# Feed-forward layers: one 512-column product for a weight's high part, with the sum's halves added outside

## The chip, the core and the metric

One core of a Trainium2 chip runs the whole kernel as one program. The metric is the device time of one execution in microseconds. TensorE (PE) multiplies; VectorE (DVE), ScalarE (ACT) and GpSimd (POOL) do the rest; SyncE (SP) issues most of the DMA.

## The reference

Two transformer blocks over 256 tokens of width 1024 (float32). The first block has two layers, each a feed-forward layer, a mixing layer (a causal convolution, then latent attention), and a second feed-forward layer. The second block mixes tokens by a gated recurrence and attention over a context, and ends in 16 experts.

```python
def swiglu_ffn(h, w1, w3, w2):
    return (jax.nn.silu(h @ w1) * (h @ w3)) @ w2

def first_block(x, ...):                # D_MODEL 1024, D_FF 2816
    h = x
    for i in range(DEPTH):              # 2
        h = h + 0.5 * swiglu_ffn(rmsnorm(h, ffn_norm1[i]), ffn1_w1[i], ffn1_w3[i], ffn1_w2[i])
        m = rmsnorm(h, mix_norm[i])
        h = h + (conv_module(m, ...) if i % 2 == 0 else mla(m, ...))
        h = h + 0.5 * swiglu_ffn(rmsnorm(h, ffn_norm2[i]), ffn2_w1[i], ffn2_w3[i], ffn2_w2[i])
    return rmsnorm(h, final_norm)
```

So there are four feed-forward layers; each reads 3 x 1024 x 2816 weights.

## The kernel before

**Products in three parts.** A float32 product is made of float32r products: the weight is split into a high part whi and a low part wlo, the activation into xh and xl, and `mm3` adds whi xh (L301), whi xl (L302) and wlo xh (L303) in one PSUM region. Features lie on partitions, the 256 tokens along the free axis, and a [128, 128] tile of the weight is stationary, so each product has 256 moving columns and the three of a triple load the stationary operand three times.

**The weights' stream.** `Stream` loads chunks of up to 1 MB, mostly [128, 8, 256], into a ring of raw buffers in the order of use. A chunk is used in two parts. For each part ScalarE copies the high part (L193, whi) and VectorE subtracts for the low part (L197, wlo); four pairs of buffers hold parts ahead of their use, and a part's pair is refilled when TensorE is through with it. These splits are issued between the products, and so stand in the queues of ScalarE and VectorE at written-out places.

**A feed-forward layer** (`ffn`, L551). For each of 11 pairs of hidden blocks there is a gate projection pg (w1) and an up projection pu (w3): two column blocks of 128, 8 k each, into one PSUM bank [128, 2 x 256] (`proj_pair`). Then VectorE multiplies pg by rb, the tokens' 1 / rms (L569), ScalarE takes Silu (L570), GpSimd multiplies by rb again (L571), VectorE multiplies with pu (L573), and `split_act` makes hh on ScalarE (L338) and hl on VectorE (L340). `out_proj` (L527) then takes 22 k for 8 output blocks, two at a time, each in a bank of its own (pd). For each output block `done` adds it to h on VectorE (L491; L489 in the mixing layers; L1174 in the last layer), and makes the next layer's xh (L492) and xl (L493).

**Order.** The schedule is as written: each engine works its instructions in program order. Fillers, small pieces of other work such as the second block's context, are put at set places (`FILL1`, `FILL3`: after each hidden pair, after each output block). Among them are the context's transposes, four turns of a bank ctr (L1060) that VectorE reads twice each (hc, L1063).

**PSUM.** Of eight banks, five take turns for products (`bank`), two serve small sums (`psx`) and one the conditions and the like (`psf`). A tile waits for the last reader of the tile that had its bank before.

Of the kernel before, what the change touches and what calls it, by code (L numbers as in the profile page):

```python
# [17 lines left out]
P = 128  # L18
# [7 lines left out]
# vectors brought in as rows of 128 and transposed on the chip: name -> first row, rows  # L26
# [10 lines left out]
# f32 inverse frequencies, ROPE_THETA ** (-2 i / 64) and ROPE_THETA ** (-2 i / 32)  # L37
# [4 lines left out]
def hmask(p):  # L42
    """pairs (s, c) of a 32 x 32 block that halves of blocks of 2, 4, ... 32 split, both ways"""
    s, c = p[:, None] % 32, np.arange(32)[None, :]
    lv = []
    for b in (1, 2, 4, 8, 16):
        same = s // (2 * b) == c // (2 * b)
        lv.append(same & (s // b < c // b))
        lv.append(same & (s // b > c // b))
    return np.concatenate(lv, 1).astype(np.float32)  # L50


def constants():
    """Arrays that depend on shapes alone, side by side in one [128, n] array."""
# [76 lines left out]
class Chunk:  # L131
    """A piece of a weight, [128, k, f]; its split parts are used in order, once each."""
# [6 lines left out]
    def parts(self):  # L139
        """(first k, number of k, (hi, lo)) for each part"""  # L140
# [5 lines left out]
class Stream:  # L146
    """Weights in the order in which they are used: loaded as far ahead as the rings have room,
    and those for float32r products split into a high and a low part, n_hl parts ahead."""
# [15 lines left out]
    def add_ring(self, pool, n):  # L164
        """n more buffers"""
        self.rings.append([pool, n, 0])
# [16 lines left out]
    def spare(self):  # L183
        """a buffer, when all is loaded"""
# [22 lines left out]
    def ahead(self, n):  # L207
        """the high parts of the next n splits, where they are loaded; -> what makes the low ones"""
# [29 lines left out]
    def drop(self):  # L238
        """the chunk that was got last is used up"""
# [9 lines left out]
    def get(self, k, f, load, split=True):  # L249
        """the next chunk; all that were got before are used up"""  # L250
# [11 lines left out]
def wcols(name, idx, c0, n, k0=0, nk=None):  # L262
    """Chunk: rows k0*128.. (nk tiles), columns c0..c0+n of a [K, N] weight."""
# [11 lines left out]
def wq_heads(g):  # L275
    """Heads 2g and 2g+1 of the query weight: 128 + 128 columns without, 64 + 64 with rotation."""
# [8 lines left out]
def two(a):  # L285
    """[128, 512] as [128, 2, 256]"""
# [3 lines left out]
class Kernel:  # L290
# [8 lines left out]
    def mm3(self, ps, w, x, start, stop, **kw):  # L299
# [3 lines left out]
        mm(ps, w[1], x[0], start=False, stop=stop, **kw)  # L303

# [30 lines left out]
    def split_act(self, hi, lo, src, scale=1.0):  # L335
        """scale * src (f32) -> hi + lo in float32r, exactly (scale: a power of two)."""
# [33 lines left out]
    def rstd_from_sum(self, sums, n, c=2):  # L370
        """sums [128, c] (PSUM or SBUF): -> [128, c] of 1 / sqrt(sum / n + eps)"""
# [4 lines left out]
    def warm(self, func):  # L376
        """brings in the function's table"""
# [3 lines left out]
    def rsqrt(self, m, c):  # L381
# [4 lines left out]
        # one Newton step takes the square root's table to float32's accuracy  # L386
# [24 lines left out]
    def bcast(self, r, dg=None):  # L411
        """r [128 tok, 2] -> [128, 256] with r along the free axis, in PSUM"""
# [7 lines left out]
    def apply_norm(self, src, rb, gain, xh, xl, nk, func=None, shift=None, new=None):  # L420
        """func(src[:, k] * gain(k) * rb) or that + shift(k) -> hi + lo"""
# [23 lines left out]
    def new_act(self):  # L445
        xh = self.actp.tile([P, KD, T], F32R, name="xh", tag="xh")
        xl = self.actp.tile([P, KD, T], F32R, name="xl", tag="xl")
        return xh, xl
# [1580 lines left out]
```

## Time and profile before

| | |
|---|---|
| time, median of 3 runs | 1829.04 us (1826.76 to 1830.6) |
| span of the profiled execution | 1826.4 us |
| mean granted TensorE clock | 0.937 |
| first feed-forward layer | about 11 to 218 us |
| convolution | about 218 to 399 us |
| second and third feed-forward layer | about 399 to 782 us |
| latent attention | about 782 to 900 us |
| fourth feed-forward layer | about 900 to 1091 us |
| second block up to the experts | 1091 to 1340 us |
| experts | 1340 to 1826 us |

The stages' ends are read from the first matmul of each. A granted clock of 1.00 is TensorE's upper level, 2.4 GHz. A matmul's record is longer than the distance to the next one's start, since matmuls are pipelined; what one costs in a dense stretch is the distance of the starts. In a row, the text in square brackets is the idle time before the instruction and what ended it.

### The profile page before, as it was taken

Reading aid. Unit: us, or ns where it says so; the run is one execution under the profiler, and the core shown is the slowest. Engines: PE = TensorE matmul, PEld = TensorE weight load, DVE = VectorE, ACT = ScalarE, POOL = GpSimd, SP = SyncE. Lnnn points to the kernel's source line nnn. Section 1 sums busy time; section 2 is a strip of 40 time slices with the busy share of each in tenths; the row PEclk is TensorE's granted clock in tenths of the full one; section 3 lists DMA queues with packets and bytes.
Section 4 is the critical chain, followed back from the end, with each engine's and each line's share of the span. In section 5 each row is a group of like instructions: output and inputs, shape, how many; then the busy total and the mean of one; then the engine's idle time right before and its main releaser. Section 6 shows DMA issues by size and latency. Waiting matters only on the chain.

```text
span 1826.4 us, 32080 instructions
## 1 busy us (share of the span) xinstructions
PE 1628.4 (89%) x13567; PEld 1376.9 (75%) x13567; DVE 921.3 (50%) x1470; ACT 696.2 (38%) x1082; POOL 229.2 (13%) x222
## 2 busy tenths in 40 slices
PE   8999989799999999999999999988988866766765
PEld 8998988689999999987999999877973421322322
DVE  5555689965555655564665536876641110101101
ACT  5454465464444544444544445545431000000001
POOL 0112067411100111010011020310010000000000
PEclk9999998899999999999999999999988988877876
DMA  8767733335556565566755558332889999999997
GB/s 266 224 225 261 227 119 113 94 112 182 184 175 201 164 197 174 172 191 221 226 175 183 172 181 252 106 99 80 307 330 372 408 409 409 409 409 408 409 409 279
DMA packets 262891, 435.40 MB, mean 238 GB/s; under 512 B 15466, under 2 KB 203548, under 8 KB 260700
## 3 DMA queue, kind: packets, MB, share of 16 engines
q1 hardware_dynamic: 262188, 431.52, 67.3%
q8 instruction: 106, 1.74, 0.4%
q0 software_dynamic: 528, 1.84, 0.3%
q14 instruction: 37, 0.30, 0.1%
q10 hardware_dynamic: 32, 0.01, 0.0%
HBM read 432.27 MB, written 1.05 MB: 237 GB/s over the span
## 4 chain that ended last, share of the span: by engine, by line
PE 59%; DMA 23%; DVE 13%; ACT 3%; issue 2%; SPq 0%; POOL 0%; DVEq 0%; ACTq 0%; POOLq 0%
DMA raw<-in_w_exp_up_dram 16%; PE mm L301 12%; PE mm L303 12%; PE mm L302 12%; DMA raw<-in_w_exp_down_dram 6%; PE pd L301 6%; PE pd L302 6%; PE pd L303 6%; DVE cv L663 4%; DVE wlo L197 2%; PE gu L1725 1%; ACT whi L193 1%; PE mod L948 1%; PE xe L1684 1%; DMA raw<-in_ffn_w_dram 0%
## 5 line engine op out<-in xcount | busy, mean ns | idle before, releaser
L197 DVE TENSOR_TENSOR wlo<-raw,whi 128x1024 fp32r<-128x1024 f32 (+1 forms) x381 | 456.9, 1224 | 203.4 <-ACT whi L193 202.5
L303 PE MATMUL mm<-xh,wlo 128*128 128x256 f32 (+1 forms) x1888 | 537.4, 285 | 6.6 <-DVE wlo L197 6.6
L301 PE MATMUL mm<-xh,whi 128*128 128x256 f32 (+1 forms) x1888 | 540.1, 286 | 3.3 <-ACT whi L193 3.0
L302 PE MATMUL mm<-xl,whi 128*128 128x256 f32 (+1 forms) x1888 | 537.1, 284 | 0.4 <-DVE xl L431 0.3
L193 ACT ACTIVATE whi<-raw 128x1024 fp32r<-128x1024 f32 (+1 forms) x381 | 382.3, 1031 | 190.2 <-PE mm L302 83.7
L301 PEld LDWEIGHTS mm<-xh,whi 128*128 128x128 f32 (+1 forms) x1888 | 364.7, 193 | 9.1 <-ACT whi L193 3.6
L303 PEld LDWEIGHTS mm<-xh,wlo 128*128 128x128 f32 (+1 forms) x1888 | 364.4, 193 | 8.0 <-DVE wlo L197 8.0
L302 PEld LDWEIGHTS mm<-xl,whi 128*128 128x128 f32 (+1 forms) x1888 | 364.6, 193 | 0.8 <-DVE xl L431 0.5
L1725 PE MATMUL gu<-raw,xe 128*32 128x512 f32 x1024 | 158.4, 718 | 59.6 <-DMA raw<-in_w_exp_up_dram 59.5
L301 PE MATMUL pd<-hh,whi 128*128 128x256 f32 x704 | 199.6, 284 | 1.3 <-DVE hc L1063 1.3
L302 PE MATMUL pd<-hl,whi 128*128 128x256 f32 x704 | 199.2, 283 | 0.0
L303 PE MATMUL pd<-hh,wlo 128*128 128x256 f32 x704 | 199.2, 283 | 0.0
L1725 PEld LDWEIGHTS gu<-raw,xe 128*32 128x32 f32 x1024 | 26.4, 116 | 150.2 <-issue 144.9
L301 PEld LDWEIGHTS pd<-hh,whi 128*128 128x128 f32 x704 | 135.1, 192 | 4.0 <-issue 2.3
L302 PEld LDWEIGHTS pd<-hl,whi 128*128 128x128 f32 x704 | 135.1, 192 | 0.0
L303 PEld LDWEIGHTS pd<-hh,wlo 128*128 128x128 f32 x704 | 135.1, 192 | 0.0
L1737 DVE TENSOR_TENSOR mhd<-gu,msg 128x256 f32<-128x256 f32 x16 | 6.8, 425 | 232.3 <-ACT msg L1733 232.3
L1754 PE MATMUL dn<-raw,mht 128*32 128x256 f32 x1024 | 85.8, 489 | 32.6 <-DMA raw<-in_w_exp_down_dram 18.2
L571 POOL TENSOR_TENSOR sg<-sg,rbs 128x512 f32<-128x512 f32 x44 | 56.7, 1288 | 450.5 <-ACT sg L570 450.5
L1754 PEld LDWEIGHTS dn<-raw,mht 128*32 128x32 f32 x1024 | 35.3, 135 | 80.5 <-DMA raw<-in_w_exp_down_dram 36.0
L1733 ACT ACTIVATE msg<-gu 128x256 f32<-128x256 f32 x16 | 6.1, 383 | 219.7 <-PE gu L1725 219.7
L475 POOL TENSOR_TENSOR ssum<-ssum,sq 128x256 f32<-128x256 f32 x48 | 37.8, 794 | 362.2 <-ACT sq L474 362.2
(447 smaller groups left out, 2126.3 us busy)
## 6 DMA issues: line engine op xcount, KB each, us to landing
raw<-in_ffn_w_dram SPq DMA_DIRECT2D x120, 1024.0 KB
raw<-in_w_exp_gate_dram SPq DMA_DIRECT2D x128, 512.0 KB
raw<-in_w_exp_up_dram SPq DMA_DIRECT2D x128, 512.0 KB
raw<-in_w_exp_down_dram SPq DMA_DIRECT2D x64, 1024.0 KB
raw<-in_w_in_dram SPq DMA_DIRECT2D x28, 1024.0 KB
raw<-in_w_mod_dram SPq DMA_DIRECT2D x24, 1024.0 KB
raw<-in_ffn_w_dram SPq DMA_DIRECT2D x16, 768.0 KB
raw<-in_conv_w_pw_dram SPq DMA_DIRECT2D x12, 1024.0 KB
```

The costliest lines, as they stand in the source:

```text
L193: nc.scalar.activation(hi, r, AF.Copy)
L197: eng.tensor_tensor(lo, r, hi.bitcast(F32), op=ALU.subtract)
L301: mm(ps, w[0], x[0], start=start, stop=False, **kw)
L302: mm(ps, w[0], x[1], start=False, stop=False, **kw)
L303: mm(ps, w[1], x[0], start=False, stop=stop, **kw)
L475: (eng or nc.vector).tensor_tensor(ssum, ssum, s, op=ALU.add)
L571: nc.gpsimd.tensor_tensor(two(sg), two(sg), rb, op=ALU.mult)
L663: self.nc.vector.scalar_tensor_tensor(acc, src, g, acc, op0=ALU.mult, op1=ALU.add)
L948: nc.tensor.matmul(ps[32 * j:32 * j + 32, :n], self.crep[:, min(c0, 1), k0 + k], w[:, k, n * j:n * j + n], start=k0 + k == 0, stop=k0 + k ...
L1684: nc.tensor.matmul(ps, nat[:, t, k * P:(k + 1) * P], oh[:, t], start=t == 0, stop=t == 1)
L1725: nc.tensor.matmul(pg[32 * j:32 * j + 32], xe[:, k, slots], w[:, :, 256 * j:256 * j + 256], start=k == 0, stop=k == KD - 1)
L1754: nc.tensor.matmul(pd[32 * g:32 * g + 32, :T], ht[:, i, 32 * j:32 * j + 32], w[:, i, 256 * g:256 * g + 256], start=j == 0 and i == 0, stop ...
```

## The change

In the feed-forward layers the two products with whi become one: xh and xl now lie side by side in one tile [128, k, 2, 256], so whi meets 512 moving columns and leaves whi xh in the first half and whi xl in the second half of a PSUM bank; wlo xh is added to the first half (`mm2`). The halves are added when the sum is read: in the hidden pairs by a ScalarE copy of the second half and a VectorE addition, in `done` by one more step of h. A column block now takes a whole bank, so a pair takes two (`wide`). During the feed-forward layers PSUM's five banks become two such double banks and one single bank (`split_banks`); the pools are closed and opened at the layers' borders. The product of pg and rb moves from VectorE to GpSimd. The transposed input takes both double banks at the start, so the very first gate projection is made as before in the single bank (`one_bank`). The diff also takes comments out, which moves line numbers.

```diff
+    def mm2(self, ps, w, x, k, start, stop):
+        mm = self.nc.tensor.matmul
+        both = lambda: mm(ps, w[0], x[2][:, k].rearrange("p a t -> p (a t)"), start=start, stop=stop,
+                          skip_group_check=True)
+        low = lambda: mm(ps[:, :T], w[1], x[0][:, k], start=False, stop=False, skip_group_check=True)
+        for f in (low, both) if stop else (both, low):
+            f()
+
+    def split_banks(self, halves):
+        self.psum_of.close()
+        pool = lambda n, b: self.psum_of.enter_context(self.tc.tile_pool(name=n, bufs=b, space=PSUM))
+        self.psw = pool("psw", 2) if halves else None
+        self.psum = pool("psum", 1 if halves else 5)
+
+    def wide(self, name="mw"):
+        return self.psw.tile([P, 1024], F32, name=name, tag="mw").rearrange("p (m f) -> p m f", m=2)
...
     def new_act(self):
-        xh = self.actp.tile([P, KD, T], F32R, name="xh", tag="xh")
-        xl = self.actp.tile([P, KD, T], F32R, name="xl", tag="xl")
-        return xh, xl
+        return self.halves(self.actp.tile([P, KD, 2, T], F32R, name="x", tag="x"))
+
+    def halves(self, x):
+        return x[:, :, 0], x[:, :, 1], x
...
-            def done(d, ps):
+            def done(d, ps, ps2=None):
                 h, g = self.h[:, d], self.V(gname, off + d)
+                if ps2 is not None:
+                    nc.vector.scalar_tensor_tensor(h, ps2, scale, h, op0=ALU.mult, op1=ALU.add)
...
+    def proj_wide(self, w, x, nk):
+        ps = self.wide()
+        for k0, n, p in w.parts():
+            for k in range(n):
+                for m in range(2):
+                    c = slice(m * P, (m + 1) * P)
+                    self.mm2(ps[:, m], (p[0][:, k, c], p[1][:, k, c]), x, k0 + k, k0 + k == 0, k0 + k == nk - 1)
+        return ps[:, :, 0:T], ps[:, :, T:]
...
-            pd = [self.bank("pd") for _ in range(nb)]
+            if halves:
+                pw = self.wide("pw")
+                pd = [pw[:, m] for m in range(nb)]
+            else:
+                pd = [self.bank("pd") for _ in range(nb)]
...
-                r = done(d, ps[:, :T])
+                r = done(d, ps[:, :T], ps[:, T:]) if halves else done(d, ps[:, :T])
...
                 w = self.S.get(KD, 256, wcols(n1, (i,), 256 * c, 256, 0, KD))
-                pg = self.proj_pair(w, x, KD)
+                sg = self.tmp.tile([P, 512], F32, name="sg", tag="sg")
+                if c == 0 and self.one_bank:
+                    pg = two(self.proj_pair(w, x, KD))
+                else:
+                    pg, pg2 = self.proj_wide(w, x, KD)
+                    nc.scalar.activation(two(sg), pg2, AF.Copy)
+                    nc.vector.tensor_tensor(two(sg), pg, two(sg), op=ALU.add)
+                    pg = two(sg)
...
-                pu = self.proj_pair(w, x, KD)
+                pu, pu2 = self.proj_wide(w, x, KD)
                 if c == 0:
                     rb = next(late)
-                sg = self.tmp.tile([P, 512], F32, name="sg", tag="sg")
-                nc.vector.tensor_tensor(two(sg), two(pg), rb, op=ALU.mult)
+                if c == 0 and self.one_bank:
+                    self.one_bank = False
+                    nc.vector.tensor_tensor(two(sg), pg, rb, op=ALU.mult)
+                else:
+                    nc.gpsimd.tensor_tensor(two(sg), pg, rb, op=ALU.mult)
                 nc.scalar.activation(sg, sg, AF.Silu)
                 nc.gpsimd.tensor_tensor(two(sg), two(sg), rb, op=ALU.mult)
                 hd = self.tmp.tile([P, 512], F32, name="hd", tag="hd")
-                nc.vector.tensor_tensor(hd, pu, sg, op=ALU.mult)
-                self.split_act(hh[:, 2 * c:2 * c + 2].rearrange("p a t -> p (a t)"),
-                               hl[:, 2 * c:2 * c + 2].rearrange("p a t -> p (a t)"), hd)
+                nc.scalar.activation(two(hd), pu2, AF.Copy)
+                nc.vector.tensor_tensor(two(hd), pu, two(hd), op=ALU.add)
+                nc.vector.tensor_tensor(hd, hd, sg, op=ALU.mult)
+                self.split_act(hd2[0][:, 2 * c:2 * c + 2], hd2[1][:, 2 * c:2 * c + 2], two(hd))
...
-        pss = [self.bank("tr") for _ in range(4)]
+        pss = [a for _ in range(2) for a in (lambda ps: (ps[:, 0], ps[:, 1]))(self.wide("tr"))]
+        self.one_bank = True
...
     def blocks(self):
+            self.split_banks(True)
             x, sums = self.start(sp)
...
+            self.split_banks(False)
             x, sums = self.conv(x, sums, self.into("ffn_norm2", 0), sp)
```

`split_banks(True)` is also called before the second feed-forward layer (the third follows at once) and before the fourth, `split_banks(False)` before the latent attention and before the second block's mixer. In `last` (the fourth layer's `done`) h also takes two steps, and `out_proj` calls `mm2` where `halves` is set, `mm3` elsewhere.

## Rows read from the trace of the kernel before

**Rows 1.** Page, part 1: busy us, share of the span, count, by engine

```profile
PE 1628.4 (89%) x13567; PEld 1376.9 (75%) x13567; DVE 921.3 (50%) x1470; ACT 696.2 (38%) x1082; POOL 229.2 (13%) x222
```

**Rows 2.** Busy time by stretch: stretch, its length, engines, granted clock, DMA share, GB/s

```profile
2.00:200.00 198.00, 191.97 (x1551) 183.93 (x1552) 112.18 (x143) 99.41 (x129) 24.84 (x17) 1.00 0.78 253
...
200.00:406.00 206.00, 177.44 (x1164) 165.95 (x1162) 172.28 (x272) 115.06 (x235) 90.41 (x89) 0.93 0.37 116
...
406.00:597.00 191.00, 191.00 (x1595) 191.00 (x1594) 110.92 (x127) 92.09 (x112) 18.60 (x17) 1.00 0.58 182
...
907.00:1095.00 188.00, 187.82 (x1577) 186.85 (x1576) 100.28 (x114) 85.80 (x106) 24.66 (x23) 1.00 0.56 181
...
1404.00:1826.00 422.00, 290.33 (x2267) 114.52 (x2266) 53.05 (x158) 21.91 (x51) 0.53 (x1) 0.81 0.99 395
```

**Rows 3.** Timeline of TensorE, second layer: start us, length us, line, tiles

```profile
449.74 0.28 PE L303 MATMUL mm<-xh,wlo 128*128 128x256 f32 x1
...
452.98 0.28 PE L303 MATMUL mm<-xh,wlo 128*128 128x256 f32 x1
```

**Rows 4.** Groups by line: shapes xcount, busy us, mean ns, idle time before

```profile
L301 PE MATMUL mm<-xh,whi 128*128 128x256 f32 x1880 | 537.8, 286 | 3.3 <-ACT whi L193 3.0 <-ACT xh L430 0.2
...
L301 PE MATMUL pd<-hh,whi 128*128 128x256 f32 x704 | 199.6, 284 | 1.3 <-DVE hc L1063 1.3
```

**Rows 5.** Timeline of TensorE, latent attention: stationary operand of 64 columns

```profile
790.03 0.28 PE L301 MATMUL mm<-xh,whi 128*64 128x256 f32 x1
...
791.05 0.28 PE L301 MATMUL mm<-xh,whi 128*64 128x256 f32 x1
```

**Rows 6.** Chain of waits, latent attention: start us, length us, what; 512 columns

```profile
813.01 1.39 PE mm L835 x6
```

**Rows 7.** Groups by line: the durations used for added work

```profile
L197 DVE TENSOR_TENSOR wlo<-raw,whi 128x1024 fp32r<-128x1024 f32 x340 | 419.6, 1257 | 186.7 <-ACT whi L193 186.0
...
L193 ACT ACTIVATE whi<-raw 128x1024 fp32r<-128x1024 f32 x340 | 349.6, 1054 | 167.4 <-PE mm L302 81.2 <-PE pd L302 61.8 <-issue 11.1
...
L573 DVE TENSOR_TENSOR hd<-mm,sg 128x512 f32<-128x512 f32 x44 | 30.4, 692 | 98.8 <-POOL sg L571 95.8 <-PE mm L303 3.0
...
L571 POOL TENSOR_TENSOR sg<-sg,rbs 128x512 f32<-128x512 f32 x44 | 56.7, 1288 | 450.5 <-ACT sg L570 450.5
...
L1263 ACT ACTIVATE q<-mm x2: 597/597/597, 1127.6 to 1146.6; 128x512 f32<-128x512 f32 x2
...
L491 DVE SCALAR_TENSOR_TENSOR h<-pd,h x24: 415/418/425, 160.7 to 783.0; 128x256 f32<-128x256 f32 x24
```

**Rows 8.** Timeline of ScalarE in a hidden pair, second layer

```profile
438.48 0.63 ACT L338 ACTIVATE hh<-hd 128x512 fp32r<-128x512 f32 x1 [2.12 <-DVE hd L573]
...
439.02 2.00 ACT L193 ACTIVATE whi<-raw 128x1024 fp32r<-128x1024 f32 x2
```

**Rows 9.** Timelines of VectorE and TensorE, first layer: the context's transposes

```profile
201.52 2.81 DVE L1063 TENSOR_SCALAR hc<-ctr,cmodT 128x256 f32<-128x256 f32 x6
...
202.66 0.36 PE L301 MATMUL pd<-hh,whi 128*128 128x256 f32 x1 [1.30 <-DVE hc L1063]
```

**Rows 10.** Timelines of VectorE and TensorE: the input's copies, the first up product

```profile
19.56 2.48 DVE L1922 COPY h<-tr 128x512 f32<-128x512 f32 x4
...
20.39 0.36 PE L301 MATMUL mm<-xh,whi 128*128 128x256 f32 x1
```

**Rows 11.** Timelines of TensorE and VectorE: convolution to second feed-forward layer

```profile
399.06 0.28 PE L301 MATMUL mm<-xh,whi 128*128 128x256 f32 x1
...
403.02 0.42 DVE L489 TENSOR_TENSOR h<-pd,h 128x256 f32<-128x256 f32 x1
```

**Rows 12.** Timelines of TensorE and VectorE: first feed-forward layer to convolution

```profile
218.57 0.28 PE L301 MATMUL mm<-xh,whi 128*128 128x256 f32 x1
...
220.12 0.42 DVE L491 SCALAR_TENSOR_TENSOR h<-pd,h 128x256 f32<-128x256 f32 x1
```

More of the change, by code (lines that the diff above doesn't have):

```diff
@@ L525, in proj_tok, with out_proj @@
                                               stop=k0 + k == nk - 1 and j == 2, skip_group_check=True)
-    def out_proj(self, x, nk, chunks, done, blocks=(2, 2, 2, 2)):
+    def out_proj(self, x, nk, chunks, done, blocks=(2, 2, 2, 2), halves=False):
         d = 0
         for nb in blocks:
-            pd = [self.bank("pd") for _ in range(nb)]
+            if halves:
[3 more added lines that the diff above has]
+                pd = [self.bank("pd") for _ in range(nb)]
             w = nb * P
@@ L556, in ffn @@
         with self.tc.tile_pool(name="ffn", bufs=1) as fp:
-            hh = fp.tile([P, NF, T], F32R, name="hh")
-            hl = fp.tile([P, NF, T], F32R, name="hl")
+            hd2 = self.halves(fp.tile([P, NF, 2, T], F32R, name="hh"))
             for c in range(NF // 2):
                 w = self.S.get(KD, 256, wcols(n1, (i,), 256 * c, 256, 0, KD))
-                pg = self.proj_pair(w, x, KD)
+                sg = self.tmp.tile([P, 512], F32, name="sg", tag="sg")
[6 more added lines that the diff above has]
+                    pg = two(sg)
                 if c == 0:
@@ L579, in chunks @@
                 return [(wcols(n2, (i,), c, w, k0, n), k0, n) for k0, n in ((0, 8), (8, 8), (16, 6))]
-            return self.out_proj((hh, hl), NF, chunks, done(0.5, nfill[1]))
+            return self.out_proj(hd2, NF, chunks, done(0.5, nfill[1]), halves=True)
     def late_rb(self, sums):
@@ L1169, in last, with done @@
         s2 = self.sum_sq(lambda d: self.V("final_norm", d),
-                         self.actp.tile([P, KD, T], F32R, name="ssum2", tag="xh").bitcast(F32))
-        def done(d, ps):
+                         self.actp.tile([P, KD, 2, T], F32R, name="ssum2", tag="x").bitcast(F32)[:, :, 0])
+        def done(d, ps, ps2):
             h = self.h[:, d]
+            self.nc.vector.scalar_tensor_tensor(h, ps2, scale, h, op0=ALU.mult, op1=ALU.add)
             self.nc.vector.scalar_tensor_tensor(h, ps, scale, h, op0=ALU.mult, op1=ALU.add)
@@ L1379, in mixer @@
                     nc.vector.tensor_tensor(t, f(ga[c], j), f(gb[c], j), op=ALU.add)
-                    self.split_act(f(y[0], jy), f(y[1], jy), t, 0.5)
+                    self.split_act(y[0][:, jy], y[1][:, jy], two(t), 0.5)
         ring("raw1", self.N_RAW1)
@@ L1869, in run @@
                 with ExitStack() as banks:
-                    self.psum, self.psx, self.psf = (
-                        banks.enter_context(tc.tile_pool(name=n, bufs=b, space=PSUM))
-                        for n, b in (("psum", 5), ("psx", 2), ("psf", 1)))
+                    self.psx, self.psf = (banks.enter_context(tc.tile_pool(name=n, bufs=b, space=PSUM))
+                                          for n, b in (("psx", 2), ("psf", 1)))
+                    self.psum_of = banks.enter_context(ExitStack())
                     if self.blocks():
@@ L1945, in blocks @@
             return True
+        self.split_banks(True)
         x, sums = self.ffn(x, sums, 0, "ffn2_w1", "ffn2_w3", "ffn2_w2", self.into("ffn_norm1", 8))
@@ L1954, in blocks @@
                 return True
+            self.split_banks(False)
             x, sums = self.mla(x, sums, self.into("ffn_norm2", 8))
@@ L1958, in blocks @@
             return True
+        self.split_banks(True)
         x, finish = self.block2_in(*self.ffn(x, sums, 1, "ffn2_w1", "ffn2_w3", "ffn2_w2", self.last))
@@ L1965, in blocks @@
             return True
+        self.split_banks(False)
         self.mixer(x, finish)
```

7 lines of the change are left out of this document (5 added, 2 removed).

## The prediction

> **What bounds the kernel now.** I read the busy line of the page first: TensorE is busy for 89% of the span, VectorE for half, ScalarE for 38% [rows 1]. An average over stages says little, so the busy time by stretch came next [rows 2]. Three kinds of stage stand apart. In the feed-forward stretches TensorE is busy all the time (191.00 of 191.00 us in the second layer) at a granted clock of 1.00, its upper level of 2.4 GHz, with DMA at about 0.6. From 200 to 406 us, the convolution, VectorE is the fullest (172 of 206 us). From 1404 us on DMA is at 0.99: the experts' weights. Their loads start only after the mixer, and the weight stream before has room, so a microsecond won in a feed-forward layer moves the experts' stream forward by the same. I count it in full.
>
> Inside a feed-forward layer the matmuls stand in triples (L301, L302, L303). Each triple's three products start evenly: from 449.74 to 452.98 us there are 27 of them, 0.1200 us apart [rows 3]. The reader should see the start times, not the 0.28 us of a record, as neighbours overlap. Both groups together are 1,880 + 704 triples, of which the four feed-forward layers have 4 x 528 = 2,112 (22 hidden blocks x 8 k, twice, and 8 output blocks x 22 k) [rows 4].
>
> **What a product costs.** Where the stationary operand has 64 columns and not 128, the same 256 moving columns start 1.02 / 9 = 0.1133 us apart [rows 5]. So 64 more weight columns cost 6.7 ns. Taken as proportional, 128 weight columns cost 13.3 ns, and the 256 moving columns the other 106.7 ns. A product with 512 moving columns would then take 213.3 + 13.3 = 226.7 ns. The only float32r products with 512 columns in this trace take 1.39 / 6 = 231.7 ns [rows 6]; their moving operand is four pieces of 128 columns, lying apart, while the changed kernel's is 512 in one piece. So I take 226.7, from [rows 3, 5], whose moving operands are in one piece as well, and keep 231.7 as one end. The other end is the columns alone, 213.3, should the longer product hide the load altogether.
>
> **The gain.** A triple goes from 3 x 120.0 = 360.0 ns to 226.7 + 120.0 = 346.7 ns: the same 768 columns, one weight load fewer. The first chunk of the first layer keeps its 16 triples as they are, so 2,096 x 13.3 ns = 27.9 us are gained. With 231.7 it is 8.3 ns or 17.4 us; with 213.3 it is 26.7 ns or 55.9 us.
>
> A rule that speaks against this change can be weighed by [rows 3, 5]. The Trainium skill (TensorE: Matmul & The Clock Gate, "Step-by-step: what each phase is for") says that the next tile's weights load while this tile's product runs, through a read port of their own; its section "Back-to-back issue gap" gives N / 2.4 + 2.5 ns at the upper clock. By that, a load saved is worth only the 2.5 ns of one issue: 5.2 us in all, an estimate from that page. The trace does not agree: the page's form gives 109.2 ns for 256 columns where this kernel's rows have 120.0 and 113.3.
>
> **The added work on other engines.** For each of the 44 hidden pairs there are two ScalarE copies out of PSUM (0.60 us each, by the same shape), two VectorE additions (0.69 us, by L573), and the product with rb moves from VectorE to GpSimd (1.29 us, by L571) [rows 7]. Per pair, which is about 11.1 us of TensorE, ScalarE then has 4 x 1.05 + 2 x 0.60 + 2 x 0.63 = 6.7 us and VectorE 4 x 1.26 + 4 x 0.69 = 7.8 us [rows 7, 8]. Both fit; the cover is TensorE's own time. What matters is order, as each engine works its queue in turn. In the kernel before, the split of weights already queues behind hh: whi x2 starts only when hh ends at 439.1 us [rows 8], yet TensorE does not pause. By the durations of [rows 7], after the change a gate tile is free about 1.6 us after its last product (copy, addition, two handovers) and wanted back 5.5 us after it; an up tile likewise. A queued whi and wlo can add 2.3 us, which leaves 1.6 us. The weights' parts come three parts ahead (8.3 us), of which hh's chain takes about 3.6 and whi + wlo 2.3. I cost this at nothing; were that cover gone, it would be the second rival. In out_proj one more VectorE step of 0.42 us for each output block [rows 7] hides under some 7.6 us of products, but for the last.
>
> **What is not hidden.** Each item is TensorE standing still, with its bounds.
> - The context's transposes (ctr) in the first layer take four turns in one bank where they had five. Before, all ran at once, and the next product began at 202.66 us, when the first pair of hc had read its bank [rows 9]. After, the second to fourth turn each wait for the two hc (0.94 us) of the one before, plus the transposes' 0.6 us and two handovers: 1.9 us for each of the second and third. The fourth then transposes for 0.45 us. So 2 x 1.9 + 0.45 = 4.2 us later (3 to 5).
> - The first layer's up product takes the bank pair that holds the transposed input, which VectorE copies from 19.56 us on, half of it done at 20.8; the product started at 20.39 and would start at 21.0 [rows 10]: 0.7 us (0.5 to 1).
> - Convolution to second feed-forward layer: TensorE ran on at 399.06 us, while VectorE read the last output bank only at 403.02 to 403.44, behind two wlo [rows 11]. Five banks in turn put that last block into the first bank, which the new double bank covers. Its first product would wait until 403.6: 4.6 us (0 if the banks lie otherwise).
> - First feed-forward layer to convolution: the last double bank is free after both blocks' doubled steps. TensorE ran on at 218.57, the last block was read at 220.12 to 220.54 [rows 12]; with one step more for the block before it and one for itself that is 221.4, and 221.6 with the handover: 3.0 us (0 to 3).
> - The end of the fourth layer: one step of 0.42 us more in the chain to the norm [rows 7]: 0.4 us (0.4 to 1).
> - Heads of layers, and fills that put extra work into VectorE's and ScalarE's queues: the margins of 1 to 2 us may be missed here and there: 2 us (0 to 4). A fall of the granted clock after a pause of 4 us is in these bounds; the convolution's pauses go with 0.93 in [rows 2].
>
> Sum: 4.2 + 0.7 + 4.6 + 3.0 + 0.4 + 2.0 = 14.9 us, between 4 and 19. DMA counts stay as they are; SyncE's loads wait for wlo as before and move with it.
>
> **The sum.** The profiled execution's span goes from 1826.4 by -27.9 + 14.9 = -13.0 to 1813.4 us. Its median time is 1829.0, 2.6 above that span, so the time would be 1816.0.
>
> **The rivals.**
> - The 512-column product costs what [rows 6] show. Then 17.4 - 14.9 = 2.5 us are gained: 1826.5. For it: it is the only direct measurement. Against: the four pieces.
> - On the other side, slower: two double banks are too few. Five banks let VectorE lag by two projections, two double banks by one. It decides where copy and addition end more than 5.5 us after a projection's last product; each microsecond beyond, once for each of the 44 pairs, is 44 us, so 1816 + 44 = 1860 with one. For it: whi queues of 2 to 3 us behind hh [rows 8]. Against: the 1.6 us left over above.
> - The cost above the bare columns goes with moving columns and not with loads: 240 ns for 512. Then nothing is gained and 14.9 us are lost: 1843.9. Against it are the 64-column rows [rows 5] and the 231.7 ns [rows 6]. The skill's form above is of this kind, with its own estimate of about 1838.7.
> - The banks lie so that neither handover waits: the cost is 14.9 - 7.6 = 7.3 us, and the time 1808.4. For it: I infer the banks' places, no row shows them.
> - The longer product hides its load altogether: 55.9 - 14.9 = 41.0 us gained, 1788.0. Against: the 231.7 ns.
>
> **How the numbers follow.** My forecast, 1816.0, has a chance of 0.56, with its own range 1809 to 1822. The 231.7 ns case has 0.17, the free banks 0.12, the double banks too few 0.07, cost by columns 0.05 (the skill's form within it 0.02), the hidden load 0.03. A measurement of this kernel tells about 0.2% (3.7 us) from no change, so faster means under 1825.4 and slower over 1832.7. Faster: 0.55 of the forecast, 0.07 of the 231.7 case, 0.12 and 0.03, together 0.77. Same: 0.01 + 0.10 + 0.01 of the double banks = 0.12. Slower: 0.06 + 0.05 = 0.11. The range 1804 to 1830 holds the forecast, the free banks and nearly all of the 231.7 case: the gain of 27.9 with costs of 4 at its low end, the gain of 17.4 with costs of 18 at its high end; it leaves out the hidden load and the two slower cases, some 0.16.
>
> **What would show it.** In the changed kernel's timeline, a 512-column product should be followed by the next start after 0.227 us and a 256-column one after 0.120; the busy time by stretch should show a feed-forward layer some 7 us shorter (528 x 13.3 ns). The waits should name hc for ctr (about 4 us), the copies of the input in the first layer, and the last h of the convolution before the second layer. If TensorE waits for the additions of each pair, the second rival is right; if 512 columns take 0.232 or 0.240, the price of a load was wrong.

## The result: slower, by 0.7%

| | before | after |
|---|---|---|
| time, median | 1829.8 us (1826.8 to 1835.2) | 1844.1 us (1841.3 to 1847.3) |
| span of the profiled execution | 1826.4 us | 1845.5 us |
| mean granted TensorE clock | 0.937 | 0.931 |

The ratio is 1.0071, 95% interval 1.0051 to 1.0090. I had predicted 1816.0 us, in a range of 1804 to 1830, and given slower a chance of 0.11. The profiled execution of after took 1847.3 us, 3.2 above the median of after.

First the page, part 1, of after (to be held against [rows 1]): engine, busy us, share, count.

```profile
PE 1617.7 (88%) x11471; PEld 1269.5 (69%) x11471; DVE 1004.4 (54%) x1546; ACT 739.5 (40%) x1169; POOL 311.5 (17%) x265
```

TensorE issues 2,096 products fewer and is busy 11 us less, yet the span is 19 us longer: it stands still more. Where it stands still is said by the waits of TensorE in after, up to the second block (waiting tile and line, releaser: us in total, times, longest):

```profile
PE mw L308 <- DVE h L513: 6.1, 2, 4.4
...
PE mm L301 <- DVE h L515: 5.9, 2, 2.9
PE ctr L1112 <- DVE hc L1115: 5.5, 3, 3.1
PE mm L301 <- ACT whi L193: 4.6, 2, 3.7
...
PE mw L308 <- DVE h L1976: 1.8, 1, 1.8
```

Of the waits for h and hc the kernel before has one, of pd for hc, 1.3 us [rows 4]; of the wait for whi it has 3.0 us. Longer waits that before has too are left out (11.3 us for cfk in both; for wlo 7.7 in after and 7.5 in before). mw is the new double bank of a hidden pair, L308 the 512-column product, L513 and L515 the additions to h in `done`. The four waits for them stand at the four borders at which the pools are closed and opened. Timeline of TensorE in after, those four places, and the first up projection:

```profile
24.09 0.47 PE L308 MATMUL mw<-x,whi 128*128 128x512 f32 x1 [1.80 <-DVE h L1976]
...
232.71 0.51 PE L301 MATMUL mm<-x,whi 128*128 128x256 f32 x1 [2.94 <-DVE h L515]
...
420.25 0.55 PE L308 MATMUL mw<-x,whi 128*128 128x512 f32 x1 [4.36 <-DVE h L513]
...
797.24 0.35 PE L301 MATMUL mm<-x,whi 128*128 128x256 f32 x1 [2.92 <-DVE h L515]
...
918.11 0.47 PE L308 MATMUL mw<-x,whi 128*128 128x512 f32 x1 [1.75 <-DVE h L513]
```

And the timeline of VectorE in after just before two of them: the additions end at 232.56 and 420.10, and the products start 0.15 us later.

```profile
232.14 0.42 DVE L515 SCALAR_TENSOR_TENSOR h<-pw,h 128x256 f32<-128x256 f32 x1
...
419.68 0.42 DVE L513 TENSOR_TENSOR h<-pd,h 128x256 f32<-128x256 f32 x1
```

Inside the layers the change does what it says. Timeline of TensorE in after, second layer, a gate projection (first pair of lines) and an up projection (second pair):

```profile
502.27 0.40 PE L308 MATMUL mw<-x,whi 128*128 128x512 f32 x1
...
503.69 0.40 PE L308 MATMUL mw<-x,whi 128*128 128x512 f32 x1
...
541.52 0.39 PE L308 MATMUL mw<-x,whi 128*128 128x512 f32 x1
...
542.91 0.39 PE L308 MATMUL mw<-x,whi 128*128 128x512 f32 x1
```

Both pairs are four triples apart: 1.42 / 4 = 0.355 us and 1.39 / 4 = 0.348 us, where the kernel before has 0.360 [rows 3]. From the second layer's third hidden pair to its `out_proj`, 288 triples, the mean is 350.0 ns in after and 360.0 in before. So in after a triple gains 10.0 ns on the mean, not 13.3. What makes the two paces is taken up with the order within a triple, below.

With the start of the low product of a triple as the mark, the traces give the length of each part. The forecast is the prediction's own terms, by the part in which they fall. The last column is the experiment with five banks in turn, told below. All in us:

| part, up to | before | after | difference | forecast | five banks, wide |
|---|---|---|---|---|---|
| first product | 12.38 | 14.23 | +1.85 | 0 | 11.95 |
| first up projection | 8.32 | 10.17 | +1.85 | +0.7 | 7.90 |
| `out_proj` of the first layer | 125.24 | 124.86 | -0.38 | -4.5 | 123.18 |
| its last pair of blocks (ctr lies here) | 57.03 | 64.34 | +7.31 | +2.4 | 58.31 |
| convolution | 15.83 | 19.64 | +3.81 | +2.4 | 16.87 |
| second layer | 180.49 | 187.35 | +6.86 | +4.6 | 181.39 |
| latent attention (two layers) | 383.33 | 376.96 | -6.37 | -14.1 | 373.76 |
| fourth layer | 117.59 | 120.87 | +3.28 | 0 | 117.22 |
| its last triple | 191.05 | 185.52 | -5.53 | -7.0 | 185.10 |
| second block | 10.91 | 12.39 | +1.49 | +0.4 | 11.53 |
| sum | 1102.17 | 1116.33 | +14.2 | -15.1, and 2.0 for heads | 1087.21 |

The +14.2 us at the second block are the medians' difference, 14.3. What comes after it took 724.2 us in the profiled execution of before and 729.2 in that of after; of these 5.0, 3.2 are that execution's distance from its median. In the experts' stretch itself after shows what [rows 2] show of before (stretch, length, busy us of PE, PEld, DVE, ACT, POOL, granted clock, DMA share, GB/s):

```profile
424.00:600.00 176.00, 176.00 (x1011) 154.01 (x1011) 122.51 (x134) 95.37 (x123) 37.96 (x26) 1.00 0.57 180
...
1424.00:1845.00 421.00, 287.72 (x2237) 113.71 (x2228) 52.68 (x157) 21.59 (x50) 0.53 (x1) 0.80 0.99 392
```

The first of these lines, from the second layer, also answers the second rival: TensorE is busy for all of 176 us, so two double banks are enough in the steady state.

Two more views of after matter. The start, on ScalarE: the transposed input lies two to a double bank, and the readers take turns.

```profile
9.45 0.47 ACT L1969 ACTIVATE x<-tr,vec 128x256 fp32r<-128x256 f32 x1 [0.55 <-DVE x L1970]
...
11.50 0.47 ACT L1969 ACTIVATE x<-tr,vec 128x256 fp32r<-128x256 f32 x1 [0.55 <-DVE x L1970]
11.87 1.05 ACT L193 ACTIVATE whi<-raw 128x1024 fp32r<-128x1024 f32 x1
```

In before the same reads on ScalarE are one row of four, 7.76 to 9.69, and the first whi starts at 10.02, not 11.87. And the granted clock, busy time by stretch, around the pauses:

```profile
24.50:28.00 3.50, 3.50 (x13) 3.02 (x12) 2.75 (x9) 1.15 (x2) 0.00 (x0) 0.51 0.05 13
...
208.00:216.00 8.00, 5.43 (x22) 4.45 (x23) 5.30 (x11) 1.76 (x3) 0.74 (x1) 0.57 0.01 2
232.00:237.00 5.00, 4.29 (x23) 4.32 (x24) 2.24 (x4) 2.07 (x4) 1.41 (x3) 0.66 0.10 34
...
420.00:424.00 4.00, 3.75 (x13) 3.21 (x14) 1.81 (x3) 2.07 (x4) 1.15 (x2) 0.57 0.48 164
```

In before the clock is 1.00 at the same places: in the stretches 24.5 to 28, 199 to 207 (its ctr), 218 to 223 and 399 to 403. In after, too, it stays at 1.00 behind the pauses at 797 and 918 us. What a pause costs beside its own length stands in the timeline of TensorE in after, behind the border at 420 us:

```profile
421.44 0.63 PE L308 MATMUL mw<-x,whi 128*128 128x512 f32 x1
421.87 0.41 PE L310 MATMUL mw<-x,wlo 128*128 128x256 f32 x1
422.08 0.63 PE L308 MATMUL mw<-x,whi 128*128 128x512 f32 x1
```

A triple takes 0.64 us at the lower level, 1.2 GHz, 0.29 more than at the upper. Five such triples follow the border at 420 us, five (of three narrow products, also 0.64) that at 232 us, five the first up projection and four the context's transposes: 19 x 0.29 = 5.5 us.

### The profile page after: what moved, and what is told of

Read it like the earlier page. It is cut to its first block, busy times and chain, and to the rows that moved or that the text cites. A ratio compares the mean times of both kernels' runs of the same rounds, so it can differ in the third digit from the quotient of the medians.

```text
span 1845.5 us, 27940 instructions
## 1 busy us (share of the span) xinstructions
PE 1617.7 (88%) x11471; PEld 1269.5 (69%) x11471; DVE 1004.4 (54%) x1546; ACT 739.5 (40%) x1169; POOL 311.5 (17%) x265
## 4 chain that ended last, share of the span: by engine, by line
PE 57%; DMA 22%; DVE 13%; ACT 3%; issue 2%; POOL 1%; DVEq 0%; SPq 0%; ACTq 0%; POOLq 0%
PE mw L308 17%; DMA raw<-in_w_exp_up_dram 16%; PE mw L310 9%; PE pw L308 9%; DMA raw<-in_w_exp_down_dram 6%; PE pw L310 4%; DVE cv L715 4%; PE mm L301 3%; DVE wlo L197 3%; PE mm L303 3%; PE mm L302 3%; PE gu L1778 1%; PE pd L302 1%; PE pd L301 1%; PE pd L303 1%
## 5 line engine op out<-in xcount | busy, mean ns | idle before, releaser
L308 PE MATMUL mw<-x,whi 128*128 128x512 f32 x1392 | 486.8, 397 | 8.9 <-DVE h L513 6.1
L310 PE MATMUL mw<-x,wlo 128*128 128x256 f32 x1392 | 377.4, 281 | 0.8 <-DVE wlo L197 0.8
L308 PEld LDWEIGHTS mw<-x,whi 128*128 128x128 f32 x1392 | 257.5, 189 | 64.5 <-ACT sq L496 6.5
L310 PEld LDWEIGHTS mw<-x,wlo 128*128 128x128 f32 x1392 | 264.3, 190 | 8.1 <-DVE wlo L197 1.1
L308 PE MATMUL pw<-hh,whi 128*128 128x512 f32 x704 | 247.2, 397 | 0.4 <-ACT whi L193 0.4
L310 PE MATMUL pw<-hh,wlo 128*128 128x256 f32 x704 | 192.9, 281 | 1.5 <-DVE wlo L197 1.5
L301 PE MATMUL mm<-x,whi 128*128 128x256 f32 (+1 forms) x496 | 145.2, 293 | 10.7 <-DVE h L515 5.9
L308 PEld LDWEIGHTS pw<-hh,whi 128*128 128x128 f32 x704 | 131.0, 189 | 31.6 <-issue 1.7
L303 PE MATMUL mm<-x,wlo 128*128 128x256 f32 (+1 forms) x496 | 143.2, 289 | 6.7 <-DVE wlo L197 6.7
L302 PE MATMUL mm<-x,whi 128*128 128x256 f32 (+1 forms) x496 | 142.6, 287 | 0.3 <-DVE x L451 0.3
L310 PEld LDWEIGHTS pw<-hh,wlo 128*128 128x128 f32 x704 | 133.5, 190 | 4.8 <-DVE wlo L197 2.1
L301 PEld LDWEIGHTS mm<-x,whi 128*128 128x128 f32 (+1 forms) x496 | 97.3, 196 | 16.0 <-issue 6.6
L302 PEld LDWEIGHTS mm<-x,whi 128*128 128x128 f32 (+1 forms) x496 | 97.1, 196 | 0.5 <-DVE x L451 0.5
```

What stands on the lines that cost most here:

```text
L301: mm(ps, w[0], x[0], start=start, stop=False, **kw)
L302: mm(ps, w[0], x[1], start=False, stop=False, **kw)
L308: both = lambda: mm(ps, w[0], x[2][:, k].rearrange("p a t -> p (a t)"), start=start, stop=stop, skip_group_check=True)
L310: low = lambda: mm(ps[:, :T], w[1], x[0][:, k], start=False, stop=False, skip_group_check=True)
```

## The experiments

The theory after the result (A): the wide product gains its 10 ns a triple, and the rest is PSUM: banks taken in pairs, and pools closed and opened at borders. Rival (B): the wide product is itself worth little or nothing, or the added steps on ScalarE, VectorE and GpSimd hold TensorE up.

**The wide product alone undone** (e1_two). All else stays as changed.

```diff
-        both = lambda: mm(ps, w[0], x[2][:, k].rearrange("p a t -> p (a t)"), start=start, stop=stop, ...)
+        def both():
+            mm(ps[:, :T], w[0], x[0][:, k], start=start, stop=stop, skip_group_check=True)
+            mm(ps[:, T:], w[0], x[1][:, k], start=False, stop=stop, skip_group_check=True)
```

> The changed kernel, but each 512-column product is made as two of 256 columns (whi with xh, whi with xl); banks, copies and additions stay. The triples' distances in the changed kernel's trace come to 350 ns on average against 360 before. Theory A (a weight load costs about 13 ns, the waits ate the gain): this run is slower than the changed kernel (1844 us) by 2,096 x 10 ns = 20 us: 1865. Theory B (cost goes with moving columns, so the wide product gave nothing): the same as the changed kernel, 1844.

Measured: 1860.8 us, 1.0162 of before (1.0133 to 1.0191). Triples are 0.360 us apart again; timeline of TensorE, second layer:

```profile
500.12 0.28 PE L309 MATMUL mw<-x,whi 128*128 128x256 f32 x1
...
500.48 0.28 PE L309 MATMUL mw<-x,whi 128*128 128x256 f32 x1
```

The wide product is worth 16.7 us by the medians, 18.9 by the profiled spans. A holds: the gain is there, and the rest of the change costs 1860.8 - 1830.0 = 30.8 us.

**Double banks out: five single banks in turn** (e2_rot). Pools are opened once; a pair takes two banks and gives each back by itself; the halves are added in four instructions of 256 columns in place of two of 512.

```diff
     def split_banks(self, halves):
-        self.psum_of.close()
...
+        if not hasattr(self, "psum"):
+            self.psum = ...tile_pool(name="psum", bufs=5, space=PSUM)
     def wide(self, name="mw"):
-        return self.psw.tile([P, 1024], F32, name=name, tag="mw").rearrange("p (m f) -> p m f", m=2)
+        return [self.bank(name) for _ in range(2)]
+    def halves_sum(self, out, ps):
+        for m in range(2):
+            self.nc.scalar.activation(out[:, m], ps[m][:, T:], AF.Copy)
+            self.nc.vector.tensor_tensor(out[:, m], ps[m][:, :T], out[:, m], op=ALU.add)
...
-        pss = [a for _ in range(2) for a in (lambda ps: (ps[:, 0], ps[:, 1]))(self.wide("tr"))]
+        pss = [self.bank("tr") for _ in range(4)]
```

> The changed kernel with its wide products, but the five banks stay in turn for the whole of the two blocks: no pool is closed or opened, a column block takes one bank of the five, and a pair's copies and additions are made by halves (four of 256 columns in place of two of 512). Theory A (the reopened pools, the shared double bank and the single bank ate the gain): the four border waits of 12 us go, the start comes 1.8 us earlier, ctr costs about 4 us less, and some 3 us at the lower clock go with them: from 1844 to about 1823, under the kernel before. Theory B (the loss lies in the longer queues of VectorE, ScalarE and GpSimd): 1844 or more, as these get more work.

Measured: 1815.2 us, 0.9917 of before (0.9900 to 0.9934): faster than both kernels, by 28.9 us than after, and 8 us under what theory A expected. The start on ScalarE is one row again, and the waits of TensorE up to 230 us name hc once, where after had it three times:

```profile
7.73 1.93 ACT L1970 ACTIVATE x<-tr,vec 128x256 fp32r<-128x256 f32 x4 [2.80 <-PE tr L1964]
9.58 1.06 ACT L193 ACTIVATE whi<-raw 128x1024 fp32r<-128x1024 f32 x1
```

```profile
PE pw L308 <- DVE hc L1116: 1.8, 1, 1.8
...
PE mw L308 <- DVE h L1977: 0.7, 1, 0.7
```

At the borders no product waits for h. Behind its own wait for hc five triples still take 0.64 us (202 to 206 us), so what after loses there, four such triples, is not won back. The marks of the table above show where the 28.9 us lay. After stands behind this kernel by 2.3 us at the first product, 4.5 at the first up projection, 7.2 at the third pair of output blocks, 12.3 at the fourth (ctr), 15.0 at the convolution, 21.0 at the second layer, and still 21.0 at the `out_proj` of the third: inside the layers the two run alike. Then 24.2 at the latent attention, 27.8 at the fourth layer, 29.1 at the second block. The other form of the copies and additions, four of 256 columns, is part of this step and was not tried by itself; the marks leave it little, as the loss lies at the start, at ctr and at the borders.

**Both out: five banks in turn and narrow products** (e9_rot_two), the two edits above in one kernel.

> The kernel of e2_rot (five banks in turn) with the 512-column product made as two of 256 with the same weight tile; the halves are still added outside. Theory A (the wide product is worth the same whatever the banks are): slower than e2_rot's 1815.2 by what e1_two lost against the changed kernel, 16.7 to 18.9 us: 1832 to 1834, triples 360 ns apart, and the halves' additions with single banks cost 2 to 4 us against the kernel before (1830.0). Theory B (part of e2_rot's gain comes from its banks and its order and not from the wide product): under 1828.

Measured: 1835.3 us, 1.0029 of before (1.0015 to 1.0044). So the wide product is worth 1835.3 - 1815.2 = 20.1 us here: A. And what is left of the change, the halves' copies and additions together with the product with rb on GpSimd, costs 5.3 us against before; by the interval of the ratio that is 2.7 to 8.1, so the 2 to 4 expected are not refuted. In its trace 2.9 of the 4.6 us by which its second block starts late are gathered in the first layer, where the fills lie, and 0.6 in the second and third layer together.

The four kernels divide the loss into three steps. That the steps add up is arithmetic, since each starts where the one above it ends; each is a difference of two medians and good to some 4 us (the median of before beside the experiments is 1830.0):

| from | to | step | us |
|---|---|---|---|
| before, 1830.0 | five banks, narrow, 1835.3 | halves kept apart and added, rb's product on GpSimd | +5.3 |
| five banks, narrow | five banks, wide, 1815.2 | the wide product | -20.1 |
| five banks, wide | after, 1844.1 | double banks, one single bank, pools closed and opened | +28.9 |

**The borders alone, in the kernel before** (e7_border). Nothing of the change but that the five-bank pool is closed and opened at the six places.

```diff
+    def reopen(self):
+        self.psum_of.close()
+        self.psum = self.psum_of.enter_context(self.tc.tile_pool(name="psum", bufs=5, space=PSUM))
...
+            self.reopen()
             x, sums = self.conv(x, sums, self.into("ffn_norm2", 0), sp)
```

> The kernel before, with nothing changed but that the pool of five banks is closed and opened again at the six places where the changed kernel does it. Theory A (the first tile of a reopened pool waits for the last reader in the closed one): TensorE waits 2.1 + 4.5 + 1.2 + 1.9 = 9.7 us at the four borders, by the last reads of h in the trace of before, and with a stretch or two at the lower clock the time goes from 1830 to about 1841. Theory B (only tiles that lie on the same bank wait): two of the borders at most, 0 to 5 us, 1830 to 1835.

Measured: 1840.2 us, 1.0052 of before (1.0035 to 1.0069), so 10.1 us for an edit that leaves every product and every bank size as it was. Waits of TensorE up to 1100 us, the additions to h being L493 and L495 here:

```profile
PE mm L301 <- DVE h L493: 6.1, 2, 4.4
...
PE mm L301 <- DVE h L495: 3.0, 2, 2.0
```

The profiled execution took 1850.1 us, 9.9 above this kernel's median; its waits are those of after, at the same four borders: 9.1 us, against 12.0 there. The difference is in the two after feed-forward layers (3.0 and 5.9), where `done` has one step fewer. The pause at the fourth layer, 1.74 us, is followed by five triples at 0.64 us, where that of after, 1.75 us, is followed by none; which pause costs a stretch at the lower clock stays open.

**Which banks lie under the new pool** (e5_swap). My prediction had the wait go with overlap: a new tile waits for what was in its bank. Opening the single bank first shifts the double banks by one.

```diff
-        self.psw = pool("psw", 2) if halves else None
         self.psum = pool("psum", 1 if halves else 5)
+        self.psw = pool("psw", 2) if halves else None
```

> The changed kernel, but at every border the single bank is opened before the two double banks, so that the next layer's first tile falls on a bank that has long been free. TensorE waits for the last h at four borders, 2.9 + 4.4 + 2.9 + 1.8 = 12 us. Theory A (the wait is for the one bank that is covered): the four waits go, and with the lower clock behind them some 14 us: 1830. Theory B (a reopened pool waits for all that was in the closed one): waits and time as in the changed kernel, 1844.

Measured: 1841.9 us, 1.0061 of before (1.0040 to 1.0083). Waits of TensorE up to 1100 us:

```profile
PE mw L308 <- DVE h L513: 6.1, 2, 4.4
PE mm L301 <- DVE h L515: 5.8, 2, 2.9
PE ctr L1112 <- DVE hc L1115: 5.5, 3, 3.1
```

Nothing moves (6.1, 5.9 and 5.5 in after). The first tile of a newly opened pool waits for the last reader of the closed pool, with the banks in another order too. No row shows the banks' places themselves; shown is that the order in which they are handed out changes nothing. That closing by itself brings the wait is what e7_border shows.

**The context's transposes in the small sums' banks** (e3_aux): ctr takes the two banks of `aux`, which alternate.

```diff
-            ps = self.bank("ctr")
+            ps = self.aux("ctr")
```

> The changed kernel, but the context's four turns of transposes take the two banks of the small sums in turn and not the single bank. Theory A (each place where TensorE stands still is worth its wait and a stretch at the lower clock): the wait of 5.5 us of ctr on hc falls to 1 to 3 us, and the time from 1844 to about 1838. Theory B (these waits are made up for by the convolution, which VectorE bounds): no change, 1844.

Measured: 1840.9 us, 1.0050 of before (1.0034 to 1.0067): 3.2 us less than after. The two intervals overlap, so the medians alone decide for neither theory; by the marks the part with ctr, from the third pair of output blocks to the fourth, went from 24.9 to 21.7 us, as much. The wait for hc is gone from TensorE's waits; those for h stay at 6.1 and 5.8. The same edit on top of the five banks (e8_rot_aux) brings nothing: 1814.6 us, 0.9923 (0.9906 to 0.9940).

> As the run with the five banks in turn, and the context's transposes on the two banks of the small sums. If the transposes still cost TensorE a wait there: 1 to 3 us under that run. If the five banks in turn cover them: the same as that run.

**The order within a triple** (e4_order, and e6_rot_order with five banks). `mm2` turns the order at the last k; here the wide product always comes first. The question was whether the turn makes the two paces, 0.355 and 0.348 us.

```diff
-        low = lambda: mm(ps[:, :T], w[1], x[0][:, k], start=False, stop=False, skip_group_check=True)
-        for f in (low, both) if stop else (both, low):
+        low = lambda: mm(ps[:, :T], w[1], x[0][:, k], start=False, stop=stop, skip_group_check=True)
+        for f in (both, low):
```

> The changed kernel, but the 512-column product always comes before the 256-column one, also at the end of a sum, where the changed kernel turns the two round. In the changed kernel's trace some chunks run at 347 ns a triple and others at 353, and the change between them falls on the ends of sums. If the turned pairs set that: all triples at one of the two, 347 (time about 1837) or 353 (about 1851). If the distance hangs on where operands lie: gate chunks 353 and up chunks 347 as before, 1844.

> As the run with the five banks in turn, and the 512-column product always first. With the order alone the feed-forward layers' triples took 347 ns more often, and the median time did not move. If the order is worth what the distances say: 3 to 7 us under the run with the five banks in turn, about 1818. If not: the same as that run.

Measured: 1844.3 us (1.0076, 1.0052 to 1.0100) and 1815.4 us (0.9915, 0.9898 to 0.9931): by the medians no difference from after and from e2_rot. The triples did change. Timeline of TensorE in e6_rot_order, second layer, two starts that lie 16 triples apart, with the end of a projection between them:

```profile
470.33 0.39 PE L308 MATMUL mw<-x,whi 128*128 128x512 f32 x1
...
475.88 0.39 PE L308 MATMUL mw<-x,whi 128*128 128x512 f32 x1
```

That is 5.55 / 16 = 0.347 us. Over the 288 triples that have a mean of 350.0 ns in after and in e2_rot, the mean is 346.7 in e4_order and in e6_rot_order, and there is one pace and not two. So the turn at the last k makes the two paces, and a triple without it takes the 346.7 ns that I had forecast. The second and third layer together, from first to last triple, took 370.5 us in e4_order and 373.2 in after, 370.9 in e6_rot_order and 373.2 in e2_rot, and the second block begins 4.6 and 4.5 us earlier. The pace that the first expectation names came true, its time of 1837 did not. Why the medians don't show the gain stays open: what comes after that point took 727 to 734 us in these four profiled executions, which is more spread than the gain.

**The product with rb back on VectorE** (e10_rot_dve), on top of five banks.

```diff
-                    nc.gpsimd.tensor_tensor(two(sg), pg, rb, op=ALU.mult)
+                    nc.vector.tensor_tensor(two(sg), pg, rb, op=ALU.mult)
```

> The kernel of e2_rot with the product of the gate and rb on VectorE, as in the kernel before, and not on GpSimd. Theory A (the slowed VectorE and GpSimd instructions lie beside TensorE's work): within 4 us of e2_rot's 1815.2; the mean of wlo (128x1024) falls from about 1.30 towards 1.26 us and that of the remaining GpSimd product from 1.5 towards 1.3 us. Theory B (the slowing reaches TensorE): faster, 1811 or less. Theory C (VectorE's queue becomes too long): slower than 1820, with waits of TensorE for hd or wlo.

Measured: 1812.6 us, 0.9916 of before (0.9883 to 0.9949), beside 0.9917 for e2_rot: no difference by the medians, though the wide interval alone would not exclude theory B's 4 us. What moves is the duration of the instructions (groups by line; first the two of e2_rot, then the two of this kernel):

```profile
L197 DVE TENSOR_TENSOR wlo<-raw,whi 128x1024 fp32r<-128x1024 f32 x340 | 449.6, 1344 | 153.3 <-ACT whi L193 153.0
...
L624 POOL TENSOR_TENSOR sg<-sg,rbs 128x512 f32<-128x512 f32 x44 | 73.1, 1661 | 96.1 <-ACT sg L623 96.1
```

```profile
L197 DVE TENSOR_TENSOR wlo<-raw,whi 128x1024 fp32r<-128x1024 f32 x340 | 418.3, 1253 | 143.6 <-ACT whi L193 143.1
...
L624 POOL TENSOR_TENSOR sg<-sg,rbs 128x512 f32<-128x512 f32 x44 | 56.8, 1291 | 438.4 <-ACT sg L623 438.4
```

With one product fewer on GpSimd, wlo falls from 1,344 to 1,253 ns and the product that stays from 1,661 to 1,291, nearly the values of before [rows 7]; none of the 340 wlo now overlaps a product of GpSimd's in a hidden pair, where in e2_rot 78 do. From the second layer to the latent attention TensorE needs 373.6 us here and 373.8 in e2_rot, and in neither does it wait there for wlo, sg or hd. So inside the layers A holds: the slowing lies beside TensorE's work.

## Why the prediction was wrong, step by step

The prediction was -27.9 + 14.9 = -13.0 us; the kernels gave -20.1 + 28.9 + 5.3 = +14.1.

- **"Taken as proportional, 128 weight columns cost 13.3 ns"**, and so 346.7 ns for each of the 2,096 triples. The price of a triple was right, the step to all triples was not: it takes them as alike, while `mm2` turns the order at the end of each sum, which I put at nothing. The mean is 350.0 ns with the turn, and 346.7 without it (e4_order, e6_rot_order). The gain is 2,096 x 10.0 = 21.0 us by the pace and 20.1 by e2_rot and e9_rot_two. Missing: 7 to 8 us. Inside the triple the sum is better than its parts: in e6_rot_order the next start comes 230.0 ns after the wide product, nearer to the 231.7 of [rows 6] than to 226.7, and 116.7 after the narrow one, for which I had 120.0. The third rival, cost by columns, falls with e1_two; that its 1843.9 us lie next to the measured 1844.1 is chance.
- **"Five banks in turn put that last block into the first bank, which the new double bank covers."** Behind the two borders that I costed, and the two that I did not, stands the rule that a new tile waits for what lay in its bank. This failed. I booked 4.6 + 3.0 us at two borders and nothing at the latent attention and the fourth layer. All four waited: 4.4 + 2.9 + 2.9 + 1.8 = 12.0 us. The two that I booked came out at their size by luck: I had priced the last read of h, and that is what a newly opened pool waits for at any border. The other two were thought away by a guess at the banks' places, which e5_swap shows to play no part. That guess also gave the rival of the free banks its 0.12.
- **"A fall of the granted clock after a pause of 4 us is in these bounds"**. Too small. Four pauses, of 1.8 us (at 24), 5.5 in three pieces (ctr), 2.9 (at 232) and 4.4 (at 420), were followed by triples at the lower level; the 19 slow ones are 5.5 us, nearly three times the 2.0 (0 to 4) that stood for this and for all heads and fills together.
- **The start**, costed at 0.7 us for the up projection's wait alone. I overlooked that two halves of one double bank are one tile, so that ScalarE and VectorE read it in turn: 1.85 us at the first product and 1.85 more to the first up projection.
- **ctr**, 4.2 us (3 to 5). Nearly right in size: from the first transposing to the next product it took 8.5 us in after (204.49 to 213.02) and 3.2 in before (199.45 to 202.66 [rows 9]), so 5.3 later. The waits are not spread as I had them, though. The second turn's is 3.1 us long, as VectorE comes to the first hc only at 207.06 us, behind other work; those of the third and fourth are 1.2 each. Undoing it gave 3.2 us.
- **The halves' additions**, costed at nothing in the steady state, 0.4 at the end and part of the 2.0 for heads. The steady state was right: the narrow kernel with five banks has 360.0 ns a triple, like before. The 5.3 us of e9_rot_two lie mostly in the first layer with its fills; which fill meets which queue was not settled.
- **"I count it in full"**, of what is won before the experts, agrees with this pair: the +14.2 us at the second block are the 14.3 of the medians. It is not shown in general: the 4.6 and 4.5 us of e4_order and e6_rot_order are in no median.

Of the 27 us between forecast and result, then, some 8 are missing from the gain (the turned order: 7 us by the pace, 2,096 x 3.3 ns, 4.5 given back by the second block where it was undone), 16 the double banks and pools (28.9 against 4.2 + 0.7 + 4.6 + 3.0 = 12.5), and 3 the additions (5.3 against 2.4).

## What to carry to other kernels

Price a new allocation as well as a new instruction: closing a tile pool and opening another made the next layer's first product wait for the very last read of the old one, 10.1 us in a kernel in which nothing else was changed. Keep banks small and in turn where several readers share them; the same product that lost 14 us in double banks won 15 in single ones. And a price worked out for the steady pattern holds where the pattern holds: the triple cost the forecast 346.7 ns in the two kernels that kept one order, and 350.0 on the mean where the order was turned at the end of each sum.

## What the runs showed of the hardware

**What a product costs above its columns depends on the clock.** At the upper level it is more than the columns: 120.0 ns for 256 columns in a row of such products (106.7 by 2.4 GHz) and 230.0 for 512 in e6_rot_order (213.3). At the lower level nothing is left over: three narrow products and a wide with a narrow one both take 0.64 us, 768 columns by 1.2 GHz. So the wide product gains nothing there. The Trainium skill (TensorE: Matmul & The Clock Gate, "Wait — 56ns, not 53.3ns?") has a start-to-start distance of exactly the columns at the lower level, which the trace bears out, and 2.5 ns more than the columns at the upper. Here it is 13.3 ns more for 256 columns and 16.7 for 512.

**VectorE and GpSimd slow each other.** Timeline of VectorE and of GpSimd in after: two wlo alone, and two beside the GpSimd products.

```profile
471.95 2.37 DVE L197 TENSOR_TENSOR wlo<-raw,whi 128x1024 fp32r<-128x1024 f32 x2 [0.26 <-ACT whi L193]
...
475.40 3.46 DVE L197 TENSOR_TENSOR wlo<-raw,whi 128x1024 fp32r<-128x1024 f32 x2 [0.26 <-ACT whi L193]
```

```profile
475.22 1.30 POOL L620 TENSOR_TENSOR sg<-sg,rbs 128x512 f32<-128x512 f32 x1 [6.40 <-DVE sg L608]
...
478.20 1.82 POOL L622 TENSOR_TENSOR sg<-sg,rbs 128x512 f32<-128x512 f32 x1 [1.67 <-ACT sg L621]
```

Two splits of the same shape took 2.37 us alone and 3.46 us here, and the second GpSimd product 1.82 us where the first took 1.30. The Trainium skill (SBUF — State Buffer, "Who interferes with whom") states that a VectorE instruction with two inputs in SBUF contends with a GpSimd instruction that reads SBUF, which agrees. The same section of the Trainium skill has it, for VectorE's two-port modes, that the engine that comes second is blocked for the whole of the other's instruction. Here the first of the two splits took 2.20 us and not 1.22, so it lost 0.98 us where 1.12 lay beside a GpSimd product that had begun before it; the second GpSimd product lost 0.52 us where 0.66 lay beside a split that had begun before it. That is most of the shared time, and not quite all.
